# Cache pages read through the page table and transferred by GpSimd instead of SyncE, in a one-core decoder-layer kernel

## The chip, the cores and the metric

The kernel is one program on one core of a Trainium2 chip. The metric is device time in microseconds (us), the median of several runs. A profile of one execution stands beside it. The names of the engines are those of the profile: PE is TensorE (PEld its weight loads), DVE is VectorE, ACT is ScalarE, POOL is GpSimd, SP is SyncE. SPq and POOLq are the streams in which SP and POOL issue their transfers (DMAs).

## What is computed

One layer of a hybrid decoder for a prompt of 256 tokens and a sample group of 8 sequences with 4 tokens each, 288 tokens in all, with shared weights:

```
h   = rms_norm(x, g_pre);  z = h @ w_in -> q, k, v, u, vg
A   = block-sparse attention(q, k, v);  B = spatial gating(u, vg)
mix = (sigmoid(h Wg_a) * (A Wa) + sigmoid(h Wg_b) * (B Wb)) @ w_o
x   = x + rms_norm(mix);  x = x + rms_norm(swiglu(rms_norm(x)))
x   = x + (p @ w_ple) * sigmoid(rms_norm(x) @ w_ple_gate)
```

The sample group attends to a past of 2048 positions for each of its sequences. That past lies in a paged cache in HBM:

```
past_k = cache_k[page_table]      # (8, 16 pages) -> 8 x 2048 positions, 8 heads of 128
past_v = cache_v[page_table]
```

A page has 128 positions x 8 heads x 128 values in float32, which is 512 KB. There are 16 pages of K and 16 of V for each of the 8 sequences, 256 pages in all.

## The kernel before

**Products.** Every dense product (`product`) takes weights in pieces of 512 KB (`wr`, 128 partitions x 1024 values, four slices of the contraction by 256 columns). `split` loads a piece by a DMA of SP into one of WR = 4 buffers, ACT rounds it to a high part (`wh`, L250), DVE subtracts to get the low part (`wl`, L252), and PE runs three matmuls for each slice and half of the columns: L278 and L279 with `wh`, L280 with `wl`. A piece is thus 24 matmuls of 288 columns.

**Order of the work.** The program is written as generators which `weave` interleaves by nominal costs, and a scheduler then orders each engine's instructions; each engine runs its own list strictly in order. First come three groups of q at once (`q3`, accumulators `q_107` to `q_136`), which start as the pieces of x arrive; then the fourth group of q (`q_616`, `q_617`), k, v with the prompt's attention, the gating, the gates (`gb`, `b`, `ga`), and behind those `a`, `o`, the feed-forward part (`fa`, `fg`, `f`) and the last gate (`pg`). `r0` (L228, L196 to L203) is the reciprocal norm of x, by which the accumulators of q are scaled (L336) and then rotated (`rope`, L338 to L341).

**The cache.** `cache_gen` goes through 32 rounds. A round loads two quads (four pages each) into two of BIG = 3 tiles of 2 MB (`kt` for K, `vt` for V), and multiplies the two quads of the round ahead: `score_products` (L664) for a `kt`, `value_products` (L765) for a `vt`. A tile is free again when its products are done. The rounds are interleaved with k, v, gating and gates. `query` (L652) and `own_products` (L679) copy queries on POOL, `qrp` (L638) spreads them on PE, and `values_out` (L792) writes the attention result into `A`, from which `ahl` (L866, L867) makes the operand of the product `a`.

**How a page is loaded.** `page_load` reads the page's number from the table in SBUF (`pt_sb`) into a register of the issuing engine (TENSOR_LOAD and two register instructions, L625), computes the address (one more, L626) and issues the DMA. Two orders are asked for: a page's number is read only behind the page DMA four before it, and each of the first 12 behind a certain weight load:

```python
if len(issued) < FIRST:
    st.enter_context(tc.issue_after(loads[14 + len(issued)].ins))
```

`issue_after` orders instructions of one and the same engine; the weight loads in `loads` are SP's. DMAs of SP count on eight semaphores in turn (DMAHW0 to 7) and those of POOL on eight others (DMASW0 to 7); a DMA waits until the DMA that had its semaphore before has landed.

Of the kernel before, what the change touches and what calls it, by code (L numbers as in the profile page):

```python
# [25 lines left out]
NPG = PAST // PAGE  # L26
# [5 lines left out]
NPOOL = 160  # L32
# [93 lines left out]
def tile_hybrid_step(ctx: ExitStack, tc: tile.TileContext, a: dict, o: list):  # L126
    nc = tc.nc
# [48 lines left out]
    pt_sb = p_kv.tile([1, NB * NPG], I32, name="pt_sb")  # L176
# [439 lines left out]
    issued = []  # L616

    def page_load(src, quad, i, dst, view):
        b, t = quad // QUADS, 4 * (quad % QUADS) + i
        with ExitStack() as st:  # L620
            if len(issued) >= 4:
                st.enter_context(tc.issue_after(issued[-4].ins))
            if len(issued) < FIRST:
                st.enter_context(tc.issue_after(loads[14 + len(issued)].ins))
            r = nc.sync.value_load(pt_sb[0:1, b * NPG + t:b * NPG + t + 1], min_val=0, max_val=NPOOL - 1)  # L625
        issued.append(nc.sync.dma_start(dst, view(src[bass.ds(r, 1)])))  # L626

    def q_parts():

# [118 lines left out]
    def load(kind, tile, quad, i):  # L748

        if kind == "k":  # L750
            page_load(ck, quad, i, tile[:, i], lambda pg: pg.rearrange("o p c -> (o p) c"))
        else:
            page_load(cv, quad, i, tile[i::4], lambda pg: pg.rearrange("o (a j) c -> j (o a) c", j=32))
# [491 lines left out]
```

## Time and profile before

| | us |
|---|---|
| median of 3 runs (1681.4 to 1685.34) | 1682.32 |
| the profiled execution, its own time | 1683.71 |
| its span | 1681.9 |
| PE busy | 1666.1 (99%) |
| DVE busy | 937.4 (56%) |
| ACT busy | 748.6 (45%) |
| POOL busy | 93.4 (6%) |
| bytes moved, mean rate | 414.78 MB, 247 GB/s |
| queue of SP (q1) | 409.67 MB, 70.3% of the 16 DMA engines' span |
| queue of POOL (q0) | 2.49 MB, 0.4% |

The granted TensorE clock was 1.00 in the whole execution. The profiled execution took 1.39 us more than the median of the runs, and 1.81 us lie around its span. In rows of the profile, "idle before <-" names what ended an engine's idle time, and "DMA share" is the mean busy share of the 16 DMA engines, which reads up to 1.04 when they are full.

### The profile page before, as it was taken

How to read it: one execution, taken by the hardware profiler on the slowest of the kernel's cores; microseconds unless marked ns; L12 is line 12 of the kernel's file. 1: busy time of each engine (PE TensorE's matmuls, PEld its weight loads, DVE VectorE, ACT ScalarE, POOL GpSimd, SP SyncE). 2: the span in 40 equal slices, each digit the busy share in tenths (PEclk: the TensorE clock that was granted, in tenths of full speed). 3: DMA queues.
4: the chain of work that ended last, by engine and by line, in shares of the span. 5: the costliest groups of instructions: out<-in, count | busy, mean ns of one | idle time of the engine just before them, and what ended most of it. 6: DMA issues, size and time to landing. Idle time of an engine off the chain costs nothing.

```text
span 1681.9 us, 37855 instructions
## 1 busy us (share of the span) xinstructions
PE 1666.1 (99%) x15628; PEld 1625.9 (97%) x15628; DVE 937.4 (56%) x1338; ACT 748.6 (45%) x1040; POOL 93.4 (6%) x153
## 2 busy tenths in 40 slices
PE   9999999999999999999999999999999999999998
PEld 9999999999998989999999999999999999999998
DVE  6864537544434347645855555444555555444785
ACT  6325535443424344545544444443444443444653
POOL 1110022000001000011000000000000000011000
PEclk9999999999999999999999999999999999999999
DMA  9699999999999996555555555666555555566463
GB/s 343 232 392 333 369 391 341 385 392 374 360 383 372 368 357 226 188 176 167 173 178 179 180 180 178 175 181 179 184 181 178 179 181 179 177 176 199 142 203 128
DMA packets 117086, 414.78 MB, mean 247 GB/s; under 512 B 13264, under 2 KB 14928, under 8 KB 116784
## 3 DMA queue, kind: packets, MB, share of 16 engines
q1 hardware_dynamic: 115776, 409.67, 70.3%
q8 instruction: 122, 2.00, 0.5%
q0 software_dynamic: 848, 2.49, 0.4%
q14 instruction: 52, 0.43, 0.1%
q10 hardware_dynamic: 288, 0.19, 0.0%
HBM read 407.46 MB, written 4.85 MB: 245 GB/s over the span
## 4 chain that ended last, share of the span: by engine, by line
PE 90%; DVE 4%; DMA 2%; ACT 1%; SPq 1%; issue 1%; POOL 0%; DVEq 0%; ACTq 0%; POOLq 0%
PE fg L279 5%; PE fg L278 5%; PE fg L280 5%; PE fa L279 5%; PE fa L280 5%; PE fa L278 5%; PE f L280 5%; PE f L279 5%; PE f L278 5%; PE values L765 3%; PE scores L664 3%; PE o L280 2%; PE o L279 2%; PE o L278 2%; PE gb L278 2%; PE gb L279 2%
## 5 line engine op out<-in xcount | busy, mean ns | idle before, releaser
L252 DVE TENSOR_TENSOR wl<-wr,wh 128x1024 fp32r<-128x1024 f32 (+1 forms) x497 | 601.2, 1211 | 596.9 <-ACT wh L250 586.5
L250 ACT CAST wh<-wr 128x1024 fp32r<-128x1024 f32 x499 | 514.8, 1033 | 786.3 <-PE f L279 130.9
L280 PE MATMUL f<-dhl,wl 128*128 128x288 f32 x704 | 201.4, 286 | 0.7 <-DVE wl L252 0.7
L278 PE MATMUL f<-dhl,wh 128*128 128x288 f32 x704 | 201.4, 286 | 0.0
L279 PE MATMUL f<-dhl,wh 128*128 128x288 f32 x704 | 201.3, 286 | 0.0
L279 PE MATMUL fa<-zhl,wh 128*128 128x288 f32 x688 | 195.8, 286 | 0.1
L280 PE MATMUL fa<-zhl,wl 128*128 128x288 f32 x688 | 195.7, 286 | 0.0
L279 PE MATMUL fg<-zhl,wh 128*128 128x288 f32 x680 | 194.2, 286 | 0.0
L280 PE MATMUL fg<-zhl,wl 128*128 128x288 f32 x680 | 194.2, 286 | 0.0
L278 PE MATMUL fa<-zhl,wh 128*128 128x288 f32 x688 | 193.9, 286 | 0.0
L278 PE MATMUL fg<-zhl,wh 128*128 128x288 f32 x680 | 193.3, 286 | 0.0
L280 PEld LDWEIGHTS f<-dhl,wl 128*128 128x128 f32 x704 | 133.1, 189 | 1.0 <-DVE wl L252 1.0
L278 PEld LDWEIGHTS f<-dhl,wh 128*128 128x128 f32 x704 | 133.1, 189 | 0.1
L279 PEld LDWEIGHTS f<-dhl,wh 128*128 128x128 f32 x704 | 133.1, 189 | 0.0
L279 PEld LDWEIGHTS fa<-zhl,wh 128*128 128x128 f32 x688 | 129.9, 189 | 0.3 <-DVE zhl L1062 0.3
L280 PEld LDWEIGHTS fa<-zhl,wl 128*128 128x128 f32 x688 | 129.8, 189 | 0.0
L278 PEld LDWEIGHTS fa<-zhl,wh 128*128 128x128 f32 x688 | 128.9, 189 | 0.0
L279 PEld LDWEIGHTS fg<-zhl,wh 128*128 128x128 f32 x680 | 128.5, 189 | 0.0
L280 PEld LDWEIGHTS fg<-zhl,wl 128*128 128x128 f32 x680 | 128.5, 189 | 0.0
L278 PEld LDWEIGHTS fg<-zhl,wh 128*128 128x128 f32 x680 | 128.1, 189 | 0.0
L278 PE MATMUL ga<-hhl,wh 128*128 128x288 f32 x256 | 73.9, 289 | 0.5 <-ACT wh L250 0.5
L279 PE MATMUL gb<-hhl,wh 128*128 128x288 f32 x256 | 73.7, 288 | 0.0
(349 smaller groups left out, 3717.5 us busy)
## 6 DMA issues: line engine op xcount, KB each, us to landing
wr<-in_w_ffn_in SPq DMA_DIRECT2D x176, 512.0 KB, 4.6
kt<-in_cache_k SPq DMA_DIRECT2D x128, 512.0 KB, 7.8
vt<-in_cache_v SPq DMA_DIRECT2D x128, 512.0 KB, 6.7
wr<-in_w_ffn_out SPq DMA_DIRECT2D x80, 512.0 KB, 3.6
wr<-in_w_in SPq DMA_DIRECT2D x77, 512.0 KB, 7.2
wr<-in_w_gate SPq DMA_DIRECT2D x64, 512.0 KB, 8.1
wr<-in_w_o SPq DMA_DIRECT2D x32, 512.0 KB, 4.7
wr<-in_w_ple_gate SPq DMA_DIRECT2D x32, 512.0 KB, 4.7
```

Of the source, the lines that this page charges most:

```text
L250: nc.scalar.copy(wh[:, :n], raw[:, i:i + n])
L252: nc.vector.tensor_tensor(wl[:, :n], raw[:, i:i + n], wh[:, :n], ALU.subtract)
L278: nc.tensor.matmul(accs[t], ws[i][0][:, c], xh, start=k == 0, stop=False)
L279: nc.tensor.matmul(accs[t], ws[i][0][:, c], xl, start=False, stop=False)
L280: late["mm"] = nc.tensor.matmul(accs[t], ws[i][1][:, c], xh, start=False, stop=k == n - 1)
L664: i = nc.tensor.matmul(sp[b][32 * g:32 * g + 32, 4 * n:4 * n + 4], Q[:, h2, g, dq], kt[:, :, c:c + 32], start=h2 == 1 and dq == 0, stop=h2 ...
L765: i = nc.tensor.matmul(oa[b // 4][32 * g:32 * g + 32], pt[:, c:c + 32], v[:, :, g], start=first and part == 3, stop=False)
```

## The change

```diff
         with ExitStack() as st:
             if len(issued) >= 4:
                 st.enter_context(tc.issue_after(issued[-4].ins))
             if len(issued) < FIRST:
                 st.enter_context(tc.issue_after(loads[14 + len(issued)].ins))
-            r = nc.sync.value_load(pt_sb[0:1, b * NPG + t:b * NPG + t + 1], min_val=0, max_val=NPOOL - 1)
-        issued.append(nc.sync.dma_start(dst, view(src[bass.ds(r, 1)])))
+            r = nc.gpsimd.value_load(pt_sb[0:1, b * NPG + t:b * NPG + t + 1], min_val=0, max_val=NPOOL - 1)
+        issued.append(nc.gpsimd.dma_start(dst, view(src[bass.ds(r, 1)])))
```

The 256 page numbers are read by POOL, and the 256 page DMAs are issued by POOL, so that they run in POOL's queue and count on POOL's eight semaphores. SP keeps the weights, the constants and the outputs y. In the built program SP has 548 rows where it had 1572, and POOL 1116 where it had 90 (runs of equal instructions are one row). The scheduler also orders some instructions of the other engines anew.

At the start of the program, SP before, with the constants of the attention (`kcst`), weight pieces (`wr`) and the first pages (`kt`):

```order
L315 DMA kcst<-in_c_perm 128x452 [waits DMAHW5_49]
L242 DMA wr<-in_w_in 128x1024 [waits DMAHW6_49,DVE_49]
L242 DMA wr<-in_w_in 128x1024 [waits DMAHW7_49,DVE_49]
L625 TENSOR_LOAD pt_sb [waits DMASW0_49]
L625 ISA x2
L242 DMA wr<-in_w_in 128x1024 [waits DMAHW0_49,DVE_49]
L625 TENSOR_LOAD pt_sb
L625 ISA x2
L626 ISA
L626 DMA kt<-in_cache_k 128x1024 [waits DMAHW1_49]
```

and POOL now, from its last MEMSET on (`kt_794` and `kt_903` are the two cache tiles that are free from the start, `qs` the copy of the sample group's q, `qo0` its spread form; "..." stands for further rows of the same kinds):

```order
L631 MEMSET po_581 128x128
L625 TENSOR_LOAD pt_sb_85 [waits DMASW0_49]
L625 ISA x2
...
L626 DMA kt_794<-in_cache_k 128x1024
...
L626 DMA kt_903<-in_cache_k 128x1024 [waits DMASW0_49]
...
L850 COPY qs_576<-A_572 128x256 [waits DVE_49]
L679 COPY qo0_585<-qs_576 128x4x4 [waits Pool_49]
...
L626 DMA kt_1015<-in_cache_k 128x1024 [waits DMASW1_49,PE_49]
```

The first eight pages stood on SP one by one behind weight loads; on POOL they stand behind the MEMSETs and wait only for the page table (DMASW0).

At the end of the three first q groups, DVE before, where `wl_621` is the low part of the first weight piece of the fourth q group:

```order
L252 TENSOR_TENSOR wl_533<-wr_530,wh_532 128x1024
L252 TENSOR_TENSOR wl_621<-wr_618,wh_620 128x1024
L252 TENSOR_TENSOR wl_651<-wr_648,wh_650 128x1024
L197 TENSOR_TENSOR r0t_524<-r0_104 128x288
L198 SCALAR_TENSOR_TENSOR r0t_524<-r0p_521,r0t_524 128x288
```

and now:

```order
L252 TENSOR_TENSOR wl_533<-wr_530,wh_532 128x1024
L197 TENSOR_TENSOR r0t_524<-r0_104 128x288
L198 SCALAR_TENSOR_TENSOR r0t_524<-r0p_521,r0t_524 128x288
L202 TENSOR_SCALAR r0t_524<-r0t_524 128x288
L203 TENSOR_TENSOR r0_104<-r0_104,r0t_524 128x288
L336 TENSOR_TENSOR A_572<-q0_107,r0_104 128x288
L336 TENSOR_TENSOR A_572<-q1_108,r0_104 128x288
L336 TENSOR_TENSOR A_572<-q0_121,r0_104 128x288
L336 TENSOR_TENSOR A_572<-q1_122,r0_104 128x288
L336 TENSOR_TENSOR A_572<-q0_135,r0_104 128x288
L252 TENSOR_TENSOR wl_621<-wr_618,wh_620 128x1024
```

`wl_621` went behind the four instructions of `r0` and five scalings of accumulators.

At the end of the cache, PE's last value products (L765) and the sequences' own values (L774), in the last group of `ga`, as the difference from before to now:

```order
 L279 MATMUL ga_10284<-hhl,wh 128x288
 L280 MATMUL ga_10284<-hhl,wl 128x288
+L765 MATMUL values<-vt,pt 32x256 x32
+L774 MATMUL values<-vo,pto 32x256 x4
 L278 MATMUL ga_10285<-hhl,wh 128x288
 L279 MATMUL ga_10285<-hhl,wh 128x288
```

They moved back by 40 matmuls of `ga`, and so did L792: between it and the first matmul of `a` there were 72 matmuls, and now there are 33. The other products with pages stand within 5 us of work from where they were in PE's list.

## The prediction

> **What bounds the kernel now.** I read the busy time by stages first.
>
> ```profile
> 0.00:20.00 20.00, 17.55 (x114) 16.54 (x115) 12.38 (x23) 15.20 (x27) 5.99 (x13) 1.00 0.87 309
> 20.00:75.00 55.00, 55.00 (x442) 54.63 (x441) 47.63 (x70) 24.91 (x29) 4.74 (x9) 1.00 0.78 279
> 75.00:205.00 130.00, 129.87 (x1622) 124.12 (x1621) 71.92 (x134) 57.22 (x106) 16.98 (x49) 1.00 0.95 358
> 205.00:450.00 245.00, 244.37 (x2932) 229.37 (x2931) 127.15 (x222) 106.60 (x150) 30.11 (x49) 1.00 0.99 378
> 450.00:610.00 160.00, 156.45 (x1820) 145.15 (x1819) 72.31 (x115) 58.63 (x69) 4.67 (x8) 1.00 0.98 374
> 700.00:1682.00 982.00, 972.86 (x7902) 969.64 (x7901) 546.14 (x688) 443.03 (x606) 30.95 (x26) 1.00 0.56 176
> ```
>
> The columns are the stretch, its length, busy time (and count) of PE, PEld, DVE, ACT and POOL, granted clock, DMA share, GB/s. PE is the bound everywhere; it idles 2.45 us before 20 us and not at all from there to 75. The cache's rounds lie in the rows from 75 to 610: there the DMA engines are nearly full too (0.95 to 0.99). The last row, which the change does not touch, gives the price of a dense matmul: 972.86 / 7902 = 0.123 us, so a weight piece of 24 is 2.95 us. Next, what PE waits for between 60 and 650 us:
>
> ```profile
> PE b L280 <- DVE wl L252: 1.5, 2, 0.8
> PE ga L280 <- DVE wl L252: 1.0, 2, 0.5
> PE lnp L506 <- POOL lns L518: 0.6, 1, 0.6
> PE ga L278 <- ACT wh L250: 0.5, 1, 0.5
> PE b L278 <- ACT wh L250: 0.5, 2, 0.3
> ```
>
> 4.1 us in all, 3.5 of it for weights. SP's own waits and the chain that ended last say why weights were late:
>
> ```profile
> SPq L626 <- PE values L765: 74.1, 26, 5.6
> ...
> 587.03 0.60 SPq L626
> 587.74 8.05 DMA wr<-in_w_gate
> ```
>
> A page at the head of SP's list waited for a cache tile 26 times, 74.1 us in all, and weight loads stood behind it: this one was issued after eight pages and took 8.05 us. So the stall that the change can remove is at most 4.1 us, 0.24% of the time; the rest of PE's idle time lies at the ends and behind the cache.
>
> **Part 1: weights no longer stand behind pages. Gain 3.5 us (bounds 0 and 4.1).** SP loses all 256 reads and 256 page DMAs. A weight load then waits for its own buffer alone, 4 pieces or 11.8 us of PE work ahead. I take the four rows on weights whole. The row on `lns` is POOL's own chain: 17 us of PE's list now lie between the two `lnp`, 8 before, so POOL has room for the page issues set into it.
>
> **Part 2: the first eight pages. Cost 6.0 us (bounds 0 and 10).** The rows of the start:
>
> ```profile
> 10.00:20.00 10.00, 8.75 (x66) 8.03 (x65) 8.45 (x13) 9.58 (x16) 0.00 (x0) 1.00 1.02 405
> ...
> 7.01 0.20 POOL L631 MEMSET po<- 128x128 f32 x1
> ...
> L625 SPq TENSOR_LOAD <-pt_sb x256: 260/267/492, 20.0 to 606.7; - x128
> L625 SPq FUSED_REGOPS  x256: 147/152/181, 20.5 to 607.1; - x128
> ...
> 22.04 0.88 SPq L626 DMA_DIRECT2D kt<-in_cache_k  x2
> ...
> 13.16 1.82 ACT L212 ACTIVATE hhl<-x,gains 128x288 fp32r<-128x288 f32 x4 [0.42 <-DMA x<-in_x]
> ...
> 15.97 0.39 PE L278 MATMUL q<-hhl,wh 128*128 128x288 f32 x1 [0.56 <-ACT wh L250]
> ...
> 17.23 0.51 PE L280 MATMUL q<-hhl,wl 128*128 128x288 f32 x2 [0.50 <-DVE wl L252]
> ...
> wr<-in_w_in SPq DMA_DIRECT2D x8, 512.0 KB, 7.2
> x<-in_x SPq DMA_DIRECT2D x3, 576.0 KB, 9.3
> ...
> kcst<-in_c_perm SPq DMA_DIRECT2D x1, 226.0 KB, 9.2
> ```
>
> Pages began at 22.04 us, when x had landed. Nothing holds them on POOL after its last MEMSET at 7.2: four reads of about 0.44 us, then one page after the other, the first bytes at about 10. From 10 to 20 us SP's queue alone filled the engines (share 1.02, 405 GB/s, 395 KB a us), and PE was waiting for it: the x piece for slices 4 to 7 landed at 13.16, PE resumed at 15.97. Eight pages are 4096 KB, 10.4 us of full rate. Taking that 13.16 as 1.4 us behind the last byte (11.8), the bytes of what follows end, at 1.30 us a weight piece and 1.46 an x piece, at 13.1, 14.4, 15.7 (weights), 17.1 (x), 18.4 (weights), 19.9 (x), and with the two constants at 21.9 the next weights. If two queues with work share equally, each us after 10 becomes two, until the pages are through at 10 + 20.7 = 30.7: first piece 16.2, fourth 26.8, fifth 32.3. With 1.4 us to land and 1.03 for ACT's cast PE can start them at 18.6, 29.2 and 34.7. Before, it started the fifth at 15.97 + 0.5 + 4 x 2.95 = 28.3. That is 6.4 later; with the pages' first bytes at 10.7 it is 5.7, so 6.0. No row shows the sharing. If SP's queue went first the cost is 0, if the pages did, up to the 10 us of their bytes; between these I take the equal share, since neither queue is ahead in any row. [...]
>
> **Part 3: the order on DVE. Cost 2.1 us (bounds 0 and 3).**
>
> ```profile
> 40.36 1.13 PE L228 MATMUL r0p<-x,ones_d 128*128 128x288 f32 x4
> ...
> 41.53 0.50 ACT L196 ACTIVATE r<-r0p,eps 128x288 f32<-128x288 f32 x1
> ...
> 42.66 0.45 DVE L197 TENSOR_TENSOR r0t<-r 128x288 f32<-128x288 f32 x1
> ...
> 44.48 2.28 DVE L336 TENSOR_TENSOR A<-q,r 128x288 f32<-128x288 f32 x6
> 46.67 1.22 DVE L252 TENSOR_TENSOR wl<-wr,wh 128x1024 fp32r<-128x1024 f32 x1
> ```
>
> `wl_621` now follows `r0`. On the clock of before: ACT ends at 42.03, the four `r0` steps take 44.48 - 42.66 = 1.82, five scalings 5/6 x 2.28 = 1.9, `wl_621` 1.22, so 46.97. PE, after `r0p` at 41.4, has 24 matmuls left and four of the next group that need no `wl_621`: 41.4 + 28 x 0.123 = 44.85. It waits 2.1 us, and no cover is left, as the chain starts from PE itself. Later low parts come 0.5 to 2 us ahead of need by the same count. `qrp` went 8 us forward in PE's list; `qs`, which it needs, ends 0.4 us ahead of it.
>
> **Part 4: the end. Cost 1.1 us (bounds 0 and 3).**
>
> ```profile
> 633.58 0.29 DVE L794 COPY A<-at 128x128 f32<-128x128 f32 x1 [3.01 <-PE at L792]
> ...
> 634.06 2.12 ACT L866 CAST ahl<-A 128x2304 fp32r<-128x2304 f32 x1
> ...
> 636.21 2.56 DVE L867 TENSOR_TENSOR ahl<-A,ahl 128x2304 fp32r<-128x2304 f32 x1 [0.80 <-ACT ahl L866]
> ```
>
> From the copy to the low half of `ahl` are 638.77 - 633.58 = 5.2 us. The 72 matmuls behind L792 covered 8.9; 33 cover 4.1.
>
> **Part 5: the other 248 pages. Cost 0 (bounds 0 and 13).** One round:
>
> ```profile
> 402.97 1.86 PE values L765 x32
> 404.83 1.75 PE scores L664 x64
> 420.03 1.86 PE values L765 x32
> ```
>
> A round is about 17 us, 3.6 of it products of pages, the rest 4.5 weight pieces, which take 136 of the 395 KB a us. The four `vt` pages can be issued when `values` ends (1.9), need 2048 / 259 = 7.9 us, an issue and a landing (2): 11.8 of 17. POOL's own cost per page is a read (0.44) and an issue, for which the nearest row is its 128-row store of `kT` (0.54 to 0.58): 8 x 1.0 us in 17, beside copies. Whether a page costs the DMA engines more in POOL's queue is open; the nearest rows:
>
> ```profile
> q1 hardware_dynamic: 115776, 409.67, 70.3%
> q0 software_dynamic: 848, 2.49, 0.4%
> ```
>
> 5.83 MB for a percent of the engines against 6.2 (5.5 to 7.1 by rounding): no penalty, or up to 6%. The 256 pages of 512 KB are 134 MB, and the three rows from 75 to 610 us hold 358 x 130 + 378 x 245 + 374 x 160 = 199 MB, so 6% on a page is 4% of the demand. By the DMA shares, 0.95 to 0.99 against the 1.02 of full engines, 3 to 7% is left, which just covers it. 10% on a page is 6.7% of the demand, some 1.5 to 2% of 535 us over what is left, about 8 us, or 13 with late rounds.
>
> **Sum.** 6.0 + 2.1 + 1.1 - 3.5 = +5.7 us on the profiled execution's 1683.71: 1689.4. That execution lay 1.39 above the median of the runs, so on the median 1688.0. A measurement here tells about 0.2%, 3.4 us, from no change.
>
> **The rivals.** *Early pages hidden* (SP's queue favoured, or POOL reaching its first page only near 17 us): part 2 is 0, the rest gives -0.3, no change, 1682. For it speaks that PE ran without a wait from 18 us on; against, that x itself was late by the rows above. *Faster*: SP, freed of pages, feeds PE without a gap, all 4.1 us come back, 1678; this decides only if parts 2 to 4 together stay under 0.7 us, and three separate rows speak against it. *Pages late*: POOL's queue makes pages 10% dearer, the DMA engines become the bound between 75 and 610 us; 5.7 + 8 gives 1696. *POOL locked out by DVE*:
>
> ```profile
> 75.59 0.58 POOL L367 DMA_DIRECT2D out<-kT  x1 [0.25 <-DVE kT L341]
> ...
> 75.65 1.23 DVE L252 TENSOR_TENSOR wl<-wr,wh 128x1024 fp32r<-128x1024 f32 x1 [0.38 <-ACT qr L640]
> ```
>
> If each issue had to wait out a `wl` of 1.2 us, eight pages would need 8 x 2.2 = 17.6 us and more of a 17 us round, with POOL's copies some 1.8 us over in each of 32 rounds: +58, 1740. The store above ran its 0.58 us inside a `wl`, against 0.54 for its fellows, so this hardly happens. [...]
>
> **How the numbers follow.** The sum as above 0.48 (own range 1684 to 1692, from parts 2 and 3); early pages hidden 0.27; faster 0.08; pages late 0.14; locked out 0.03. Slower 0.48 + 0.14 + 0.03 = 0.65, within 0.2% 0.27, faster 0.08. The range 1680 to 1702 leaves out the faster case, the lock and the upper end of late pages, about 0.15.
>
> **What the profile after would show.** Right: page DMAs from POOL before 10 us, the x piece of 13.16 landing near 15, PE idle 5 to 9 us in the first 50 us against 2.5; a PE wait on `wl` near `r0`; the waits of `b` and `ga` on `wl` and `wh` gone; SP without waits on `values`. Wrong: no new PE idle before 50 us (part 2 or 3 falls), or PE waits on `kt` or `vt` in most rounds, with a DMA share at 1.0 and rounds longer than 17 us (part 5 falls), which is what would carry the time past the range.

## The result and the profile after

The changed kernel takes 1694.06 us (median of 6 runs, 1691.48 to 1695.92) against 1682.49 us (median of 6). The ratio of the runs is 1.0057, 95% interval 1.0047 to 1.0068, which is +9.6 us; the two medians lie 11.6 us apart. The profiled execution took 1694.47 us, its span is 1692.8, 10.9 us longer than before. The forecast was 1688.0, slower by 5.7, in a range of 1680 to 1702: the direction came, at nearly twice the size.

The stages first, with the columns of the prediction's first view:

```profile
0.00:20.00 20.00, 16.25 (x108) 15.61 (x109) 11.55 (x22) 13.36 (x23) 10.27 (x21) 1.00 0.88 310
20.00:75.00 55.00, 47.89 (x345) 46.52 (x345) 39.34 (x59) 21.40 (x26) 0.00 (x0) 0.91 0.68 237
75.00:205.00 130.00, 129.84 (x1555) 125.17 (x1554) 73.57 (x123) 56.74 (x99) 50.66 (x106) 1.00 0.92 335
205.00:450.00 245.00, 243.14 (x2917) 228.12 (x2916) 130.24 (x238) 109.91 (x159) 82.32 (x156) 1.00 0.99 378
450.00:610.00 160.00, 158.94 (x1914) 148.67 (x1916) 77.43 (x118) 57.85 (x67) 43.67 (x89) 1.00 1.00 382
```

The row to look at is the second. Before, PE was busy in all 55 us from 20 to 75; now it is idle for 7.11 of them, and its granted clock there is 0.91 where it was 1.00. The rows of the cache's rounds hardly differ: the DMA share is 0.92 to 1.00 (0.95 to 0.99 before), and from 450 to 610 us PE idles less (1.06 us, before 3.55).

How far PE is along its list, by the first matmul of three products, before and then after (the two numbers behind the durations are the first and last start):

```profile
L278 PE MATMUL k<-hhl,wh x128: 286/286/390, 56.0 to 112.5; 128*128 128x288 f32 x128
L278 PE MATMUL b<-bhl,wh x128: 286/286/390, 451.0 to 516.4; 128*128 128x288 f32 x128
L278 PE MATMUL a<-ahl,wh x128: 286/286/286, 642.3 to 688.9; 128*128 128x288 f32 x128
```

```profile
L278 PE MATMUL k<-hhl,wh x128: 286/286/390, 69.3 to 125.4; 128*128 128x288 f32 x128
L278 PE MATMUL b<-bhl,wh x128: 286/286/391, 465.7 to 529.4; 128*128 128x288 f32 x128
L278 PE MATMUL a<-ahl,wh x128: 286/286/287, 652.9 to 701.0; 128*128 128x288 f32 x128
```

The changed kernel is 13.3 us late at k, 14.7 at `b`, 10.6 at `a`, and 10.9 at the end. More than the whole loss is made in the first 70 us, and a part of it is won back between `b` and `a`. The stretch up to k holds the same 404 matmuls in both (before, then after):

```profile
0.00:56.00 56.00, 53.55 (x404) 52.33 (x405) 41.12 (x64) 32.56 (x47) 5.99 (x13) 1.00 0.90 326
```

```profile
0.00:69.30 69.30, 58.44 (x404) 56.43 (x405) 45.26 (x70) 32.78 (x47) 10.27 (x21) 0.93 0.75 264
```

So the 13.3 us are 8.4 us of PE idle (10.86 instead of 2.45) and 4.9 us in which PE was busy longer with the same matmuls. PE's waits, with the sum, the number of times and the longest, name the idle part:

```profile
PE q L278 <- ACT wh L250: 6.4, 4, 3.8
PE q L280 <- DVE wl L252: 3.2, 3, 2.1
PE values L765 <- DMA vt<-in_cache_v: 2.8, 3, 1.1
...
PE a L279 <- DVE ahl L867: 1.1, 1, 1.1
```

and PE's timeline, the clock by stretches of 5 us, and POOL's timeline show where the rest comes from:

```profile
31.03 0.29 PE L280 MATMUL q<-hhl,wl 128*128 128x288 f32 x1
35.10 0.61 PE L278 MATMUL q<-hhl,wh 128*128 128x288 f32 x1 [3.79 <-ACT wh L250]
...
39.64 0.45 PE L280 MATMUL q<-hhl,wl 128*128 128x288 f32 x1
39.88 0.44 PE L278 MATMUL q<-hhl,wh 128*128 128x288 f32 x1
...
56.29 0.51 PE L280 MATMUL q<-hhl,wl 128*128 128x288 f32 x2 [2.08 <-DVE wl L252]
```

```profile
30.00:35.00 5.00, 1.31 (x11) 1.10 (x9) 3.41 (x6) 2.50 (x5) 0.00 (x0) 0.84 1.02 408
35.00:40.00 5.00, 4.90 (x19) 4.62 (x20) 4.92 (x5) 3.00 (x4) 0.00 (x0) 0.50 0.60 191
...
55.00:60.00 5.00, 3.71 (x19) 3.71 (x20) 5.00 (x8) 0.00 (x0) 0.00 (x0) 0.72 0.40 117
```

```profile
7.81 2.29 POOL L626 DMA_DIRECT2D kt<-in_cache_k  x4 [0.45 <-issue]
...
14.27 0.53 POOL L626 DMA_DIRECT2D kt<-in_cache_k  x1 [0.65 <-issue]
```

POOL issued all eight first pages between 7.8 and 14.8 us, although SP issued the weight loads behind which they are ordered in the program only after 18.0 us. The fifth weight piece then came late, and PE stood still before 35.10. Behind that pause PE ran at a granted clock of 0.50 until 40 us: its matmuls start 0.24 us apart (39.64 to 39.88) instead of 0.12. A second pause, the one for `wl_621` that part 3 foresaw, is followed by a second slow stretch (clock 0.72 from 55 to 60 us). In the clock's own records the first slow stretch runs from 33.35 to 40.18 us and the second from 57.25 to 60.66. PE was busy in 5.08 and 3.41 us of them, at half the clock, so that the clock accounts for 4.2 of the 4.9 us.

### The profile page after: what moved, and what is told of

The parts are those of the page before. It is cut to its first block, busy times and chain, and to the rows that moved or that the text cites. A ratio compares the mean times of both kernels' runs of the same rounds, so it can differ in the third digit from the quotient of the medians.

```text
span 1692.8 us, 37952 instructions
## 1 busy us (share of the span) xinstructions
PE 1669.5 (99%) x15628; PEld 1630.1 (96%) x15628; DVE 939.5 (55%) x1338; ACT 747.9 (44%) x1039; POOL 223.9 (13%) x409
## 4 chain that ended last, share of the span: by engine, by line
PE 72%; issue 10%; DMA 10%; DVE 4%; ACT 1%; POOLq 1%; POOL 1%; SPq 0%; DVEq 0%; ACTq 0%
DMA vt<-in_cache_v 9%; PE f L280 5%; PE f L279 5%; PE f L278 5%; PE fg L278 5%; PE fg L280 5%; PE fg L279 5%; PE fa L280 5%; PE fa L279 5%; PE fa L278 5%; PE o L280 2%; PE o L279 2%; PE o L278 2%; PE ga L278 2%; PE ga L280 2%
## 5 line engine op out<-in xcount | busy, mean ns | idle before, releaser
L918 POOL TENSOR_TENSOR ssq_fo<-ssq_fo,sq 128x288 f32<-128x288 f32 x13 | 14.9, 1148 | 769.1 <-ACT sq L916 768.7
L626 POOL DMA_DIRECT2D vt<-in_cache_v x128 | 69.7, 545 | 235.6 <-PE values L765 210.4
```

The source lines that it names most:

```text
L626: issued.append(nc.gpsimd.dma_start(dst, view(src[bass.ds(r, 1)])))
L918: nc.gpsimd.tensor_tensor(ssq[key][0], ssq[key][0], q, ALU.add)
```

## The experiments

Theory A: the start holds the whole loss, and the clock behind PE's pauses is most of what the forecast lacked. Theory B: the start costs about the 8 us that parts 2 and 3 gave it, and the rest is the price of the other 248 pages in POOL's queue. Each ratio is against the kernel before, run on the same chip.

**The first eight pages back on SP, the rest on POOL.**

```diff
+        eng = nc.sync if len(issued) < 8 else nc.gpsimd
-            r = nc.gpsimd.value_load(...)
+            r = eng.value_load(...)
-        issued.append(nc.gpsimd.dma_start(...))
+        issued.append(eng.dma_start(...))
```

> The changed kernel, with only the first eight pages back on SP behind their weight loads; the other 248 stay on POOL. Theory A (the start holds the whole loss): when PE reaches the first matmul of k the changed kernel is 13.3 us behind (69.3 against 56.0), 8.4 us more idle and 4.9 us more busy time for the same 404 matmuls; from there to the end it gains 2.4 us (span +10.9). So this one loses nothing at the start, the clock stays at 1.00 there, and it comes out 2.4 us under the kernel before: 1680 us, 1678 to 1682. Theory B (about half of the loss lies in the 248 pages of POOL's queue, as the start was only priced at 5.7 and the DVE order at 2.1): 1694.1 - 7.8 = 1686.

Measured: 1687.16 us, ratio 1.0018 (1.0009 to 1.0026), near B's 1686 and not A's 1680. The trace says why neither holds as it was written. PE, and the one wait that stands out:

```profile
L278 PE MATMUL k<-hhl,wh x128: 286/286/390, 55.8 to 118.7; 128*128 128x288 f32 x128
```

```profile
PE scores L665 <- DMA kt<-in_cache_k: 4.7, 1, 4.7
```

```profile
102.26 5.77 PE L665 MATMUL scores<-kt,qb 128*32 128x128 f32 x128 [4.73 <-DMA kt<-in_cache_k]
...
100.00:110.00 10.00, 7.74 (x144) 7.57 (x145) 2.06 (x3) 1.12 (x1) 3.38 (x9) 0.67 0.89 327
```

(The last row is of the view by stretches.) The start is whole again: k begins at 55.8 us as before, not at 69.3. The time was lost behind it, in one place: the scheduler put PE's first score products 34 dense matmuls further back than in the kernel before and the second ones 6, which leaves 65 of them between, 8 us, where there were 93. The tile that the first set free could not be filled again in that time; PE waited 4.7 us at 102, and the clock fell to 0.67 behind it. This was read from the order and the trace, and not tried by itself. The run shows that the first eight pages cause the loss of the start; it does not decide on the rest.

**All pages on POOL, the first eight behind r0.** A copy of one element of `r0` is put into POOL's list, and those pages are ordered behind it:

```diff
+    r0c = p_kv.tile([1, 1], F32, name="r0c")
+    seen = nc.gpsimd.tensor_copy(r0c, r0[:1, :1])
...
+            if len(issued) < 8:
+                st.enter_context(tc.issue_after(seen.ins))
```

> The changed kernel with all pages on POOL, and the first eight behind a copy of one element of r0 on POOL, so that none is issued before r0 is there (43 to 45 us). Theory A: no page in the first 43 us, weights and x land as in the kernel before, first k matmul near 56, time 1680 us (1678 to 1682), the same as with the first eight on SP. Theory B: 1686. A third outcome, pages too late for the first score products (81.7 us before), would show as PE waiting on kt and give some us more.

Measured: 1680.3 us (median of 11 runs), ratio 0.9981 (0.9972 to 0.9989): 3.2 us faster than the kernel before by the ratio, and the fastest of all. POOL's first page, the stage of the late rounds, PE's wait on pages, and the first matmul of `b` and `a`:

```profile
45.67 0.58 POOL L630 DMA_DIRECT2D kt<-in_cache_k  x1 [1.34 <-issue]
```

```profile
450.00:610.00 160.00, 160.00 (x1879) 149.34 (x1881) 77.26 (x119) 59.68 (x71) 41.45 (x80) 1.00 1.00 382
```

```profile
PE values L769 <- DMA vt<-in_cache_v: 0.8, 1, 0.8
```

```profile
L278 PE MATMUL b<-bhl,wh x128: 286/286/390, 451.1 to 513.6; 128*128 128x288 f32 x128
L278 PE MATMUL a<-ahl,wh x128: 286/286/286, 637.2 to 685.2; 128*128 128x288 f32 x128
```

All 256 pages run in POOL's queue, and PE has no idle time at all from 450 to 610 us, with the DMA engines full. From `b` to `a` it needs 186.1 us where the kernel before needed 191.3. Theory B is out: POOL's queue does not cost 6 us in the rounds.

**Only the first eight pages on POOL, the rest on SP.** The kernel before, with `eng = nc.gpsimd if len(issued) < 8 else nc.sync`.

> The kernel before, with only the first eight pages on POOL, where nothing holds them; the other 248 stay on SP. Theory A: the whole loss of the start and none of the later gain: +13.3 us, 1695.8 us (1693 to 1697), slower than the changed kernel itself. Theory B: only the 7.8 us or so of parts 2 and 3: 1690 or less, faster than the changed kernel.

Measured: 1696.35 us, ratio 1.0076 (1.0063 to 1.0089), where A said 1695.8. Eight DMAs of 512 KB, moved to another engine, with the orders that the scheduler then makes, cost more than the whole change. The waits are those of the changed kernel's start, with the pause for `wl` of the other DVE order among them:

```profile
PE q L278 <- ACT wh L250: 6.0, 3, 3.8
PE q L280 <- DVE wl L252: 3.2, 3, 2.1
PE ga L278 <- ACT wh L250: 2.0, 2, 1.3
```

and the wait of `ga` on weights, which the changed kernel no longer has, is still there.

**Pages on SP, without the order behind weight loads** (`FIRST` 0 instead of 12).

> The kernel before, without the order that puts each of the first 12 pages behind a weight load; all pages stay on SP. On SP they then stand closer together (three pages after weight 13, four more after the next), but still in one list behind x and the first weights. If the loss comes from a second queue that shares the engines with x and the weights (theory A), this stays within 4 us of the kernel before: 1682 to 1687, no clock dip. If it is enough that pages are asked for early, on whatever engine: 1690 or more.

Measured: 1685.45 us, ratio 1.0010 (1.0001 to 1.0019); the granted clock was 1.00 throughout. In one list the pages stand behind x and the first weights (the first at 21.4 us), so dropping the order costs little. It is the second queue, without an order, that does the harm.

**Filling PE's pause.** The changed kernel with 16 matmuls of zeros where PE waited for the fifth weight piece. They add zero to an accumulator.

```diff
+            for _ in range((fill or {}).get(k0, 0)):
+                with tc.issue_after(late["mm"].ins):
+                    nc.tensor.matmul(accs[0][:, :128], zero, ones_d, start=False, stop=False)
...
+                           fill={8: FILL} if g == 1 else None)
```

> The changed kernel with 16 extra matmuls of zeros (128x128, about 0.21 us each, 3.4 us in all) on PE ahead of the fifth weight piece, where it waited 3.8 us in the changed kernel (31.2 to 35.1) and then ran 20 matmuls at half the clock (0.24 us a matmul instead of 0.12, to 39.9). With them the schedule also puts the low part of the first piece of the fourth q group ahead of r0 again, so the 2.1 us pause at 54 and the slow 3.3 us behind it should go too. Theory A (it is the pause of PE that lowers the clock, and 4 to 5 us of the loss are the clock): the granted clock stays at 1.00 from 30 to 65 us, and the time falls by 2.4 (first dip) + 2.1 + 1.6 (second pause and dip) = 6 us: 1688. Theory B (the clock falls for another reason, the full DMA queues for instance): the clock between 33 and 40 us still reads near 0.5, and only the second pause goes: 1692 or more.

The view by stretches of 5 us, as above:

```profile
30.00:35.00 5.00, 5.00 (x46) 5.00 (x45) 3.41 (x6) 2.93 (x5) 0.00 (x0) 1.00 1.03 409
35.00:40.00 5.00, 4.25 (x35) 4.04 (x34) 4.78 (x5) 3.76 (x5) 0.00 (x0) 1.00 0.64 219
...
55.00:60.00 5.00, 5.00 (x44) 5.00 (x43) 4.93 (x11) 1.59 (x2) 0.00 (x0) 1.00 0.37 122
```

The clock stays at 1.00 while the DMA engines are as full as before (1.03 of 30 to 35 us, where the changed kernel has 1.02): with the pause of 3.8 us filled, full engines alone did not lower it. The second pause is gone for another reason: in this build the low part of the weight piece stands ahead of `r0` on DVE again. k begins at 61.3 us; 20 matmuls (2.5 us) that stood ahead of it stand behind it in this build, so the gain there is 69.3 - 61.3 - 2.5 = 5.5 us, against the 6 expected. The time of the whole did not follow: 1692.53 us, ratio 1.0059 (1.0046 to 1.0073). As in the first experiment, the two first groups of score products came closer in PE's list (72 dense matmuls between them), and PE lost 1.6 us (for a `kt`) and 2.8 us (the profile names no releaser) waiting there:

```profile
112.81 0.30 PE L671 MATMUL scores<-kt,qb 128*32 128x128 f32 x1 [2.76 <-issue]
```

The clock's part is settled by the trace, not by this total.

**The DVE order alone.** The kernel before, with the low part of the first piece of the fourth q group ordered behind the fifth scaling:

```diff
+                        if len(loads) == BEHIND:
+                            behind.enter_context(tc.issue_after(scaled[4].ins))
```

> The kernel before, with the DVE order of the change alone: the low part of the first piece of the fourth q group stands behind r0 and five scalings; pages stay on SP, where they were. Theory A (part 3 as predicted): PE waits 2.1 us for wl after r0p, near 45 us, and some 0 to 1.6 us more if the clock dips behind the pause: 2.1 to 3.7 us over the kernel before, 1685.8 to 1687.4 by the 1683.7 of this chip. Theory B (the order costs only where the weights are late already): no wait, 1683.7.

```profile
46.53 0.51 PE L284 MATMUL q<-hhl,wl 128*128 128x288 f32 x2 [2.07 <-DVE wl L256]
```

```profile
45.00:50.00 5.00, 3.47 (x28) 3.47 (x29) 5.00 (x8) 0.79 (x1) 0.00 (x0) 1.00 0.43 132
```

The wait came, with 2.07 us. This pause was not followed by a slow stretch: the clock (third number from the end) is 1.00, and stays there up to 546 us. The time is 1689.74 us, ratio 1.0028 (1.0015 to 1.0040), about 4.7 us, more than the wait. The trace has two more: 1.93 us of `qrp` for POOL's copy `qs`, and 3.0 us of `ga` for weights, where there were 0 and 0.5. The longest wait of `ga`, 2.04 us up to 544.60, is followed by a slow stretch:

```profile
546.74:550.15 3.41, 3.41 (x16) 3.13 (x15) 1.71 (x2) 2.09 (x2) 0.00 (x0) 0.50 0.59 196
```

**Four early pages instead of eight.** The gate behind `r0` holds only pages five to eight:

```diff
-            if len(issued) < 8:
+            if 4 <= len(issued) < 8:
```

> All pages on POOL as in the run with the gate behind r0, but the first four are issued at once and only the next four wait for r0. Equal sharing of packets: four pages are 5.2 us of full rate, shared from 10.0 to 20.4; the fifth weight piece can be started at about 30.9 us (28.3 without early pages, 35 with eight), PE stands still 2.6 us longer, and the clock may dip once (0 to 2.4): 1680.3 + 2.6 to 5.0 = 1683 to 1685. If pages went ahead of the weights: 5.2 us or more, 1686 to 1690. If four are hidden: 1680.

Measured: 1683.79 us, ratio 1.0002 (0.9993 to 1.0011), by the two ratios 0.21% or 3.5 us over the version that holds all eight. PE's pause and the clock:

```profile
22.61 0.39 PE L278 MATMUL q<-hhl,wh 128*128 128x288 f32 x1 [1.99 <-ACT wh L250]
```

```profile
20.00:25.00 5.00, 3.01 (x19) 2.79 (x18) 1.53 (x2) 1.92 (x4) 0.00 (x0) 0.85 1.03 416
25.00:30.00 5.00, 5.00 (x35) 5.00 (x34) 4.59 (x10) 4.99 (x10) 0.00 (x0) 0.81 1.02 388
```

The size lies in the range that equal sharing gave (2.6 to 5.0 us). The pause came one weight piece earlier than worked out, with 1.99 us instead of 2.6, and a slow stretch (23.5 to 26.9 us) followed it.

## Why the prediction was right and where it was short

**Part 2, early pages: right, 6.0 forecast.** The queues show the sharing that the prediction took without a row. Traffic of the changed kernel from 15 to 20 us, and then from 25 to 30 us (packets, MB, share of the engines):

```profile
q1 hardware_dynamic: 272, 1.02, 50.4%
q0 software_dynamic: 273, 1.01, 50.0%
```

```profile
q0 software_dynamic: 369, 1.34, 67.4%
q1 hardware_dynamic: 363, 0.67, 35.4%
```

272 packets against 273, and from 20 to 25 us 274 against 275: the two queues got nearly equal numbers of packets. It is the packets that were equal, not the bytes: from 25 to 30 us, when SP's queue carried the constants, in packets of 512 and 1808 bytes, it got 363 against 369 and half the data, 0.67 MB against 1.34. The fifth piece could be started at 35.10 us; the sum said 34.7. Of the 8.4 us of new idle time 6.3 are this part: what is left without the 2.1 of part 3.

That the two times agree so closely is in part luck. The pages' bytes ran from 12.1 to 32.8 us, not from 10 to 30.7, and ACT could start on the x piece that was to land near 15 us at 13.63; by the sum's own rule this has the fifth piece ready 0.6 us sooner. The 1.4 us that the sum took from a last byte to its landing is shown by no run: in the kernel before, the last packet of that x piece ended at 12.8 us and ACT began at 13.16. Against these stands the constants' half share of the bytes, which no term held: 0.67 MB instead of about 1.0 from 25 to 30 us, 0.8 us at the full rate. And "with the pages' first bytes at 10.7 it is 5.7" is a slip: such pages are through at 31.4 us, still ahead of the piece, and the delay stays 6.4.

**Part 3, the order on DVE: right.** 2.1 us forecast, 2.08 in the changed kernel, 2.07 with the order alone.

**The step that failed** is the end of that term, "with the pages' first bytes at 10.7 it is 5.7, so 6.0": it took a late weight piece for a pause of PE and nothing more. PE's pauses had a price behind them: 4.9 us of the 13.3 are the same matmuls taking longer, 4.2 of them by the half clock. No row of the kernel before could show that, since its longest pause for weights in this stretch was 0.56 us; but a sum that contains pauses of some us should have carried the term with a bound. The clock's records of the two traces, the kernel before and the changed one, show in what steps it came: behind the first 7 us every record but a trace's last is a whole multiple of 3.4133 us long. The kernel before has 1675.94 us at 1.00 (491 times 3.4133); the changed kernel has 27.31, 17.07 and 1631.57 us at 1.00 (8, 5 and 478 times), and 6.83 and 3.41 at 0.50 (twice and once). Its two slow stretches thus begin 23.9 us apart (33.35 and 57.25), seven times 3.4133.

How much idle time stood ahead of a slow stretch can be read in windows of this length. The window ahead of the first slow stretch of the changed kernel, the one ahead of the slow stretch in the run with the DVE order alone, and, for comparison, one with most of the pause of 2.76 us in the run with the zeros:

```profile
29.94:33.35 3.41, 1.37 (x12) 1.16 (x10) 3.21 (x6) 1.57 (x3) 0.00 (x0) 1.00 1.02 406
```

```profile
543.32:546.74 3.42, 1.64 (x11) 1.43 (x12) 1.22 (x1) 1.04 (x1) 0.00 (x0) 1.00 0.94 381
```

```profile
108.23:111.65 3.42, 1.81 (x67) 1.54 (x58) 1.07 (x2) 0.00 (x0) 2.68 (x7) 1.00 0.99 389
```

PE was idle for 2.04, 1.78 and 1.61 us; the first two windows were followed by a slow one, the third, which has 1.61 of the 2.76, was not. In the kernel before, whose clock stayed at 1.00, the most idle time that such a window has ahead of another at 1.00 is 1.75 us (1675.67 to 1679.08). So 1.78 us of 3.41 were followed by half the clock in one trace, and 1.75 were not in another. What a pause of about 2 us cost went with how it lay in these windows. The 2.08 us of the changed kernel lay in one (53.84 to 57.25), and a slow window followed, 3.41 us at clock 0.50, which is 1.7 us of lost work. The 2.07 us of the run with the DVE order alone (44.46 to 46.53) lay in two, about 0.5 and 1.55 us if the windows are counted back from that run's slow stretch at 546.74, and nothing followed.

**Part 1, weights no longer behind pages: right.** 3.5 us forecast. From `b` to `a` the changed kernel gains 4.1 us (191.3 to 187.2), the gated version 5.2, and the waits of `b` and `ga` on weights are gone from both. The changed kernel's gain is net of a new wait of 1.06 us for a page (part 5). The gated version's lies above the bound of 4.1, which counted idle time alone: with the same matmuls PE's busy time there fell as well, from 187.7 to 186.1 us.

**Part 4, the end: right.** 1.1 us forecast, 1.1 measured (the wait of `a` on `ahl`).

**Part 5, the other pages: nearly.** 0 forecast; the changed kernel has three waits of `values` on `vt`, 2.8 us, the gated one 0.8. The traffic of the whole program now:

```profile
q1 hardware_dynamic: 78912, 275.44, 49.6%
q0 software_dynamic: 37712, 136.73, 21.0%
```

Pages cost POOL's queue 6.5 MB for a percent, SP's queue has 5.6; both together take 70.6% of the engines, as before (70.7%). By these shares pages did not become dearer for the engines, but they took longer from issue to landing (median 11.0 us instead of 7.8 for `kt`, 8.3 instead of 6.7 for `vt`). The 2 us that the forecast took here for an issue and a landing stand in no row by themselves; what the rows show is 0.53 to 0.60 us for an issue, and those medians.

**The sum**, by the milestones: 6.3 + 2.1 + 4.9 to k, +1.4 to `b`, -4.1 to `a`, +1.4 over the wait on `ahl`, -1.1 to the end (a wait of `f` on weights, 0.7 us, is gone, from a stretch that the prediction took for untouched): 10.9. Without the 4.9 of longer busy time it is 6.0, against the 5.7 of the forecast; so close a sum is partly luck too, since +1.4 to `b` (waits for pages, which part 5 put at 0) and -1.1 at the end were not forecast and nearly cancel.

**The rivals.** *Early pages hidden* and *faster* are out. *Pages late* gave 1696, near the time, by a mechanism that the gated version excludes. *POOL locked out by DVE* is out: the 256 page issues took POOL 527 to 597 ns each, beside a DVE that was busy for 55% of the span.

## What to carry to other kernels

When transfers move to an engine with a queue of its own, look first for what their old place in a list held back. Here an order asked for between instructions of two engines bound nothing (the pages were issued from 7.8 to 14.8 us, the weight loads that they were to follow only from 18.0), and eight early pages shared the DMA engines with the loads that PE was waiting for, packet for packet (272 and 273 in 5 us). Give the new queue a gate of its own, such as a tiny instruction that reads a result of the right moment; here such a gate, with the order that the scheduler made around it, turned +0.57% into -0.19%. And when a sum contains a pause of TensorE of about 2 us or more, add the slow matmuls that may follow it: in these traces 0 to 1.7 us for 2 us, and 2.5 us behind the pause of 3.8.

## What the runs showed of the hardware

No pause of PE of up to 1.72 us, the longest of them in the run with the zeros, was followed by a lower clock. Of seven pauses between 1.9 and 2.8 us, over all traces, four were followed by one, for 3.4 us each (1.99 with four early pages, 2.04 with the DVE order alone, 2.08 in the changed kernel and 2.08 with only the first eight pages on POOL), and three were not (1.93 and 2.07 with the DVE order alone, 2.76 with the zeros). The three longest were too, for about 6.8 us: 3.8 in the changed kernel and with only the first eight pages on POOL, and 4.7 with those on SP and the rest on POOL; in the changed kernel 5 us of that were matmuls at half speed. The changed kernel's two slow stretches came behind a window with full and one with idle DMA engines (a share of 1.02 and of 0.02), and with matmuls of zeros in the pause the clock stayed at 1.00.
